# First early pair's Silu behind the output norm's roots, that norm's rows scaled on VectorE, three attention stores issued by ScalarE, in a hybrid encoder layer

## The chip, the cores and the metric

The kernel runs on one core of a Trainium2 chip. Times are device microseconds of one execution of the program; the time of a kernel is the median of several executions. The engines are TensorE (PE in the profile, its weight loads PEld), VectorE (DVE), ScalarE (ACT), GpSimd (POOL) and SyncE (SP), which issues most of the DMA transfers. Each engine takes its instructions from a queue of its own, in the order in which they stand there; an instruction that waits for a semaphore holds all that stand behind it on the same engine. "ACTq" and "SPq" in the profile are the queues' own steps, such as issuing a transfer.

## The reference, cut to what matters

One layer of an encoder on x of 1024 rows of 1024 numbers, all float32:

```python
h = _rms_norm(x, g_mix_pre)
aq, ak, av, dqkv, dgate, dalpha, dbeta = split(h @ w_in)
attn_o = _window_attention(rope(aq), rope(ak), av, sink)   # 8 heads of 64, 2 key heads, blocks of 128 rows
dn_o = _gated_deltanet(dqkv, dgate, dalpha, dbeta, ...)    # 4 heads of 128, both directions
x = x + _rms_norm(concat([attn_o, dn_o]) @ w_out, g_mix_post)
x = x + _rms_norm(cross_attention(_rms_norm(x, g_cross_pre), mem), g_cross_post)
gu = _rms_norm(x, g_ffn_pre) @ w_gate_up
x = x + _rms_norm((silu(gu[:, :2816]) * gu[:, 2816:]) @ w_down, g_ffn_post)
```

`_window_attention` lets each block of 128 rows see itself and its two neighbours: scores, a softmax with a sink term in the denominator, then the product with the values. `_rms_norm` divides a row by the root of its mean square.

## The kernel before

Everything is float32. A matrix product is made of three TensorE products: each operand is split into a rounded "hi" part and the rest "lo" (`split`, L103 on ScalarE makes hi, L104 on VectorE or GpSimd makes lo), and hi·hi, hi·lo and lo·hi are added up in PSUM. Weights are loaded 512 KB at a time into two buffers `wraw` and split into two buffers each of `whi` and `wlo`.

Two places are touched by the change.

**The attention windows beside the delta rule's scan.** `window(n, g)` handles the block n of 128 rows for the key head g (four query heads at once); 16 windows, counted g * NT + n with NT = 8, are run in the order 0 to 15. A window loads its queries (`qr`, L674), splits them (`qs`, L676, L677), makes the scores (`psw`, L685, TensorE), adds the band and takes the row maximum (L687, VectorE), takes the exponential (L694, ScalarE), and multiplies the four score tiles `sc` by the inverse sum `es` (L703 on VectorE or L705 on ScalarE). Its second half transposes them (`ptw`, L711), splits the transposes (`ph`, `pl`) and multiplies with the values (`pow`, L716); `ao` is the sum of two halves of that (L719 on ScalarE, L720 on VectorE) and is stored to `d_mix` (L721). There is one buffer each of `qr` and `ao`, and two PSUM buffers that `psw` and `ptw` take in turn. Windows 0 and 7, 8 and 15 stand at the edge of the sequence: their tiles are 256 wide, the others' 384. The later windows run between the steps of `scan(g)`, the delta rule for two heads in both directions: `psc` is any of its TensorE products, `kv` and `pz` are its loaded operands, L871 on VectorE makes its right-hand side R in place in `kv`, L878 and L880 make `vg` and `vn` of the next product, L891 the new state S. Between these TensorE also makes the memory's keys (`pck`, L983), whose weights GpSimd splits (L104).

**From the norm after cross attention to the feed-forward network.** Two halves of four tiles of 128 rows go through `finish(r, z, eng)`: a root for the output norm (`prs`), the residual added (`xr`, L1352, VectorE) and stored, the sum of squares of the new row (L1355, ScalarE), the root of the next norm (`pr2`, L1343 on ScalarE with the reciprocal L1344 on VectorE), and the row scaled by it (`z`): L1360 on VectorE in the second half of the rows, which is handled first, L1359 on ScalarE in the first half. The rows are then transposed on TensorE (`ptn`, L1459) and combined into sums (L1488 to L1501) that a Strassen-like product needs. While that goes on, TensorE makes five "early" pairs of columns of the gate and up products, which need only the rows that are ready: for each pair two products with the first half of the rows' columns into `pA0` (L1539, 12 matmuls each), which are copied out to `m1` (L1541, ScalarE) and stored, and two that add the second half (L1544). `early_out` then takes Silu of the gate (`sg`, L1524, ScalarE), multiplies with the up product (L1528, VectorE) and stores it. The bank `pA0` of a pair's gate or up is one of four.

ScalarE's roots (Sqrt) and Silu are in different function tables; where the function needed is not in the loaded table, an ACT_TABLE_LOAD stands ahead of it. Copies, Identity and Square are found in each.

What sets the order: the kernel is written in program order, and the builder's scheduler puts each engine's instructions into a queue by a timeline that it works out. `tc.high_priority(AHEAD)` moves the instructions in its block ahead; `tc.issue_after(x.ins)` makes those in its block stand behind x on x's engine. Eight semaphores serve the transfers of all queues in turn ("slots" below): a transfer waits until the one that had its slot eight transfers before has landed, on whichever queue that was.

Of the kernel before, what the change touches and what calls it, by code (L numbers as in the profile page):

```python
# [13 lines left out]
AF = mybir.ActivationFunctionType  # L14
ALU = mybir.AluOpType
# [6 lines left out]
D = 1024  # L22
KT = D // P
NT = S // P
# [4 lines left out]
AHEAD = 300  # L29
# [47 lines left out]
def tile_hybrid_block(  # L77
# [6 lines left out]
    nc = tc.nc  # L84
# [578 lines left out]
    def window(n, g):  # L663

        tok = slice(n * P, (n + 1) * P)
        k0, k1 = max(n - 1, 0), min(n + 1, NT - 1) + 1
        nb = k1 - k0
        w = nb * P
        band = C[:, _AT["band0"] - C0 + (k0 - n + 1) * P:][:, 0:w]

        khi, klo = (t[:, k0 * P:k1 * P] for t in keys[g])
        qr = tw.tile([P, 4, P], F32, tag="qr", name="qr", bufs=1)
        for r in range(2):
            nc.sync.dma_start(qr[64 * r:64 * r + 64], d_q[256 * g:256 * g + 256, tok].rearrange("(h e) t -> e h t", h=4))  # L674
        qs = tw.tile([P, 4, P], F32R, tag="qs", name="qs")
        nc.scalar.copy(qs, qr)  # L676
        nc.gpsimd.tensor_tensor(qs[64:128], qr[64:128], f32(qs[64:128]), ALU.subtract)  # L677

        m4 = tw.tile([P, 4], F32, tag="m4", name="m4")
        ssum = tw.tile([P, 4], F32, tag="ssum", name="ssum")  # L680
        pr = []
        for hh in range(4):
            pp = pw.tile([P, 512], F32, tag="pw", name="psw")
            for i, kk in enumerate((khi, klo)):
                nc.tensor.matmul(pp[:, 0:w], qs[:, hh, :], kk, start=(i == 0), stop=(i == 1))  # L685
            sc = tw.tile([P, 384], F32, tag="sc", name="sc", bufs=8)
            nc.vector.tensor_tensor_reduce(out=sc[:, 0:w], in0=pp[:, 0:w], in1=band, scale=0.125,  # L687
                                           scalar=sink[:, 4 * g + hh:4 * g + hh + 1], op0=ALU.add, op1=ALU.max,
                                           accum_out=m4[:, hh:hh + 1])
            pr.append(sc)  # L690
        nm = tw.tile([P, 4], F32, tag="nm", name="nm")
        nc.vector.tensor_scalar(nm, m4, -1.0, None, ALU.mult)
        for hh in range(4):
            nc.scalar.activation(pr[hh][:, 0:w], pr[hh][:, 0:w], AF.Exp, bias=nm[:, hh:hh + 1],  # L694
                                 accum_out=ssum[:, hh:hh + 1])
        es = tw.tile([P, 4], F32, tag="es", name="es")
        nc.gpsimd.tensor_tensor(es, sink[:, 4 * g:4 * g + 4], m4, ALU.subtract)
        nc.scalar.activation(es, es, AF.Exp)
        nc.vector.tensor_tensor(es, es, ssum, ALU.add)
        nc.vector.reciprocal(es, es)  # L700
        for hh in range(4):
            if not 8 <= g * NT + n < 13:
                nc.vector.tensor_scalar(pr[hh][:, 0:w], pr[hh][:, 0:w], es[:, hh:hh + 1], None, ALU.mult)  # L703
            else:
                nc.scalar.mul(pr[hh][:, 0:w], pr[hh][:, 0:w], es[:, hh:hh + 1])  # L705
        yield
        po = pw.tile([P, 4, P], F32, tag="pow", name="pow", bufs=1)
        for j in range(nb):
            pp = pw.tile([P, 512], F32, tag="pw", name="ptw")
            for hh in range(4):  # L710
                nc.tensor.transpose(pp[:, hh * P:(hh + 1) * P], pr[hh][:, j * P:(j + 1) * P], ident)  # L711
            ph = tw.tile([P, 512], F32R, tag="ph", name="ph")
            pl = tw.tile([P, 512], F32R, tag="pl", name="pl")
            split(ph, pl, pp)
            for i, pe_ in enumerate((ph, pl)):
                nc.tensor.matmul(po.rearrange("p h t -> p (h t)"), vhl[:, k0 + j, g].rearrange("p r e -> p (r e)"), pe_,  # L716
                                 start=(j == 0 and i == 0), stop=(j == nb - 1 and i == 1))
        ao = tw.tile([P, 4, P], F32, tag="ao", name="ao", bufs=1)[0:64]
        nc.scalar.copy(ao, po[64:128])  # L719
        nc.vector.tensor_tensor(ao, po[0:64], ao, ALU.add)  # L720
        nc.sync.dma_start(d_mix[g * 256:(g + 1) * 256, tok].rearrange("(h e) t -> e h t", e=64), ao)  # L721

# [614 lines left out]
        jk = tz.tile([P, HALF], F32, tag="junk", name="junk")  # L1339
        nc.scalar.activation(jk, src, AF.Square, accum_out=ssq[:, ch, r:r + 1])  # L1340

    def inverse_root(rs, ss, scale, bias):
        nc.scalar.activation(rs, ss, AF.Sqrt, bias=bias, scale=scale)  # L1343
        nc.vector.reciprocal(rs, rs)  # L1344

    def finish(r, z, eng):

        tok = slice(r * P, (r + 1) * P)
        xr = res[r]
        rs = tz.tile([P, 1], F32, tag="prs", name="prs", bufs=4)  # L1350
        inverse_root(rs, ssq[:, 1, r:r + 1], 1.0, ssq[:, 0, r:r + 1])
        nc.vector.scalar_tensor_tensor(xr, z, rs, xr, ALU.mult, ALU.add)  # L1352
        nc.sync.dma_start(d_x2[tok, :], xr)
        s2 = tz.tile([P, 1], F32, tag="ps2", name="ps2", bufs=4)
        nc.scalar.activation(z, xr, AF.Square, accum_out=s2)  # L1355
        r2 = tz.tile([P, 1], F32, tag="pr2", name="pr2", bufs=4)
        inverse_root(r2, s2, 1.0 / D, epsc)
        if eng is nc.scalar:
            return nc.scalar.activation(z, xr, AF.Identity, scale=r2)  # L1359
        return nc.vector.tensor_scalar(z, xr, r2, None, ALU.mult)  # L1360

    a11, a12, s3_, a22 = ((q_[0][:, c], q_[1][:, c]) for q_ in (q0, q1) for c in (slice(0, HK), slice(HK, KT)))
    s1_, s4_ = ([r_, [t[:, c] for t in q1]] for r_, c in zip(blocks(raw), (slice(HK, KT), slice(0, HK))))
# [65 lines left out]
        square_of(z[:, HI], 1, r)  # L1429
        gained(z[:, HI], z[:, HI], HI, nc.vector)  # L1430

    scaled = []

    def second_rows(t):
        add(za[:, t], y7[:, t], X[t])
        row_sum(zl[:, t], 4 + t)
        scaled.append(finish(4 + t, zl[:, t], nc.vector))

    def first_half_rows(t):
        add(zz[:, t, HI], e_[:, t], X[t])  # L1440
# [37 lines left out]
                    row_sum(zz[:, t], t)  # L1478
    with tc.issue_after(cut.ins):
        for t in range(4):  # L1480
            finish(t, zz[:, t], nc.scalar)
    tr = LR2.enter_context(pool("tr", 1, side="right"))
    T2, T4 = (blocks(t) for t in operand(opA, "s0"))
    T1, T3 = (blocks(t) for t in operand(opB, "s2"))
# [36 lines left out]
    te = LP.enter_context(pool("te", 2, side="right"))  # L1521

    def early_out(e, sg, A, after=None):
        nc.scalar.activation(sg, A[0], AF.Silu)  # L1524
        with ExitStack() as order_:
            if after:
                order_.enter_context(tc.issue_after(after.ins))
            nc.vector.tensor_tensor(sg, sg, A[1], ALU.mult)  # L1528
        nc.sync.dma_start(d_a["11"][e], sg)

    for e in range(EARLY):
        f = 2 * e
        w, A = [], []
        for i, c0 in enumerate((f * P, FF + f * P)):
            place = fw.tile([P, KT, P], F32, tag=f"fw{i}", name="wraw") if e == EARLY - 1 else None
            whi, wlo = first_gate[i] if e == 0 else load_w(w_gate_up[:, c0:c0 + P], KT, P, place=place)
            w.append(((whi[:, 0:HK], wlo[:, 0:HK]), (whi[:, HK:], wlo[:, HK:])))
            A.append(pg.tile([P, 512], F32, tag="pg", name="pA0"))
            product(A[i], w[i][0], X11)  # L1539
            a1 = te.tile([P, 512], F32, tag="m1", name="m1")  # L1540
            nc.scalar.copy(a1, A[i])  # L1541
            nc.sync.dma_start(d_m1[f + i], a1)
        for i in range(2):
            product(A[i], w[i][1], X21, start=False)  # L1544
# [332 lines left out]
```

## Time and profile before

| | us |
|---|---|
| median of 3 runs | 1521.06 |
| the runs | 1518.25, 1521.06, 1524.97 |
| the profiled execution, whole | 1518.84 |
| its span in the profile | 1516.8 |
| TensorE busy | 1471.5 |
| VectorE busy | 1101.3 |
| ScalarE busy | 784.2 |
| GpSimd busy | 362.8 |

The span is what the profile's rows add up to; 2.0 us of the execution lie outside it. A row of the timeline gives the start from the span's beginning, the duration, the engine, the line, the operation with its tiles (buffer numbers left out), how many instructions in a row it stands for, and, in brackets, how long the engine sat idle before it and what ended that. A row of the table by stretches gives the busy time of each engine in a stretch, the clock that TensorE was granted there (1.00 is full speed) and the share of the sixteen DMA engines' time that transfers took. The windows and the scan run from about 300 to 546 us, the passage to the feed-forward network from 841 to 945 us.

### The profile page before, as it was taken

How to read it: one execution, taken by the hardware profiler on the slowest of the kernel's cores; microseconds unless marked ns; L12 is line 12 of the kernel's file. 1: busy time of each engine (PE TensorE's matmuls, PEld its weight loads, DVE VectorE, ACT ScalarE, POOL GpSimd, SP SyncE). 2: the span in 40 equal slices, each digit the busy share in tenths (PEclk: the TensorE clock that was granted, in tenths of full speed). 3: DMA queues.
4: the chain of work that ended last, by engine and by line, in shares of the span. 5: the costliest groups of instructions: out<-in, count | busy, mean ns of one | idle time of the engine just before them, and what ended most of it. 6: DMA issues, size and time to landing. Idle time of an engine off the chain costs nothing.

```text
span 1516.8 us, 21323 instructions
## 1 busy us (share of the span) xinstructions
PE 1471.5 (97%) x7437; PEld 1239.2 (82%) x7437; DVE 1101.3 (73%) x1801; ACT 784.2 (52%) x1606; POOL 362.8 (24%) x394
## 2 busy tenths in 40 slices
PE   7999999998999999999999998999999999999998
PEld 6888877888989878887788876888888888888787
DVE  5878998676998775538466867776867764696666
ACT  7678844567556764555454684332332332453533
POOL 0011232432325303342201002433524342000030
PEclk9999999999999999999999999999999999999999
DMA  6245554557987584448625553334434333853255
GB/s 203 70 118 142 148 164 129 157 171 193 345 283 234 180 293 158 162 151 262 232 90 180 194 190 123 118 119 132 132 112 152 126 103 116 323 207 97 105 179 168
DMA packets 257751, 256.34 MB, mean 169 GB/s; under 512 B 18128, under 2 KB 190317, under 8 KB 257645
## 3 DMA queue, kind: packets, MB, share of 16 engines
q1 hardware_dynamic: 256493, 252.90, 52.3%
q10 hardware_dynamic: 1152, 2.10, 0.4%
q8 instruction: 58, 0.95, 0.3%
q14 instruction: 48, 0.39, 0.1%
HBM read 178.63 MB, written 73.70 MB: 166 GB/s over the span
## 4 chain that ended last, share of the span: by engine, by line
PE 64%; DVE 8%; DMA 5%; ACT 2%; issue 2%; POOL 1%; SPq 0%; DVEq 0%; ACTq 0%; POOLq 0%
PE pE L1514 8%; PE pD L1514 8%; PE pA L1514 6%; PE pmg L1104 6%; PE pdX L1720 6%; PE pst L1320 5%; PE pdA L1720 4%; PE pB L1514 4%; PE pcq L276 3%; PE psc L843 2%; PE pdD L1720 2%; DMA wpart<-in_w_co_dram 1%; PE pg L276 1%; DMA kv<-d_kv 1%; PE pcv L999 1%
## 5 line engine op out<-in xcount | busy, mean ns | idle before, releaser
L103 ACT CAST whi<-wraw 128x1024 fp32r<-128x1024 f32 x96 | 100.8, 1050 | 120.3 <-DMA wraw<-in_w_gate_up_dram 38.7
L276 PE MATMUL pg<-hlo,whi 128*128 128x512 f32 x352 | 140.0, 398 | 0.0
L276 PE MATMUL pg<-hhi,whi 128*128 128x512 f32 x352 | 139.4, 396 | 0.0
L276 PE MATMUL pg<-hhi,wlo 128*128 128x512 f32 x352 | 139.0, 395 | 0.0
L104 POOL TENSOR_TENSOR wlo<-wraw,whi 128x1024 fp32r<-128x1024 f32 x36 | 87.8, 2441 | 186.4 <-ACT whi L103 182.8
L1514 PE MATMUL pA<-b,whi 128*128 128x512 f32 x352 | 109.8, 393 | 3.6 <-ACT m L1541 2.8
L104 DVE TENSOR_TENSOR wlo<-wraw,whi 128x1024 fp32r<-128x1024 f32 x60 | 74.7, 1245 | 42.2 <-ACT whi L103 38.2
L1514 PEld LDWEIGHTS pA<-b,whi 128*128 128x128 f32 x352 | 65.2, 188 | 18.7 <-ACT m L1541 4.1
L1720 PE MATMUL pdX<-dhl,whi 128*128 128x512 f32 x264 | 76.1, 390 | 1.5 <-ACT dhl L103 0.8
L276 PEld LDWEIGHTS pg<-hhi,whi 128*128 128x128 f32 x352 | 66.5, 189 | 13.4 <-ACT hhi L241 0.3
L276 PEld LDWEIGHTS pg<-hlo,whi 128*128 128x128 f32 x352 | 66.5, 189 | 12.5
L276 PEld LDWEIGHTS pg<-hhi,wlo 128*128 128x128 f32 x352 | 66.5, 189 | 12.5
L1597 POOL TENSOR_TENSOR act<-act,up 128x512 f32<-128x512 f32 x33 | 51.0, 1546 | 82.0 <-DVE up L1596 60.9
L103 ACT CAST whi<-araw 128x1024 fp32r<-128x1024 f32 (+1 forms) x36 | 35.3, 981 | 67.1 <-PE pdX L1720 27.6
L1514 PE MATMUL pA<-b,wlo 128*128 128x512 f32 x176 | 68.8, 392 | 0.5 <-DVE wlo L104 0.5
L104 DVE TENSOR_TENSOR wlo<-araw,whi 128x1024 fp32r<-128x1024 f32 (+1 forms) x36 | 40.7, 1131 | 36.2 <-ACT whi L103 36.1
L1569 POOL TENSOR_TENSOR sr<-wraw 128x512 f32<-128x512 f32 x22 | 29.9, 1359 | 150.6 <-DMA wraw<-in_w_gate_up_dram 88.6
L301 DVE SCALAR_TENSOR_TENSOR acc<-cp,cols,acc 128x1024 f32<-128x1024 f32 x48 | 63.0, 1314 | 0.2
L1720 PEld LDWEIGHTS pdX<-dhl,whi 128*128 128x128 f32 x264 | 49.3, 188 | 12.7 <-ACT dhl L103 1.1
L103 ACT CAST dhl<-b 128x512 fp32r<-128x512 f32 x66 | 40.4, 620 | 31.9 <-PE pdA L1720 13.6
L1514 PE MATMUL pB<-s0h,s1h 128*128 128x512 f32 x176 | 54.4, 390 | 0.7 <-ACT s1h L103 0.7
L103 ACT CAST s0h<-sr 128x512 fp32r<-128x512 f32 x22 | 13.7, 622 | 78.7 <-POOL sr L1569 78.2
(503 smaller groups left out, 4306.1 us busy)
## 6 DMA issues: line engine op xcount, KB each, us to landing
wraw<-in_w_gate_up_dram SPq DMA_DIRECT2D x54, 512.0 KB, 3.8
kv<-d_kv SPq DMA_DIRECT2D x32, 512.0 KB, 7.2
wraw<-in_w_in_dram SPq DMA_DIRECT2D x22, 512.0 KB, 4.0
b<-in_w_down_dram SPq DMA_DIRECT2D x20, 512.0 KB, 6.3
araw<-d_as SPq DMA_DIRECT2D x20, 512.0 KB, 3.6
pz<-d_pz SPq DMA_DIRECT2D x32, 256.0 KB, 6.6
wraw<-in_w_ckv_dram SPq DMA_DIRECT2D x16, 512.0 KB, 4.7
wraw<-in_w_out_dram SPq DMA_DIRECT2D x16, 512.0 KB, 4.5
```

What stands on the lines that cost most here:

```text
L103: nc.scalar.copy(hi, src)
L104: return (eng or nc.vector).tensor_tensor(lo, src, f32(hi), ALU.subtract)
L276: nc.tensor.matmul(p_, w[:, k, :], ah[a][:, k, :], start=(k == 0 and i == 0), stop=(k == nk - 1 and i == 2))
L301: nc.vector.scalar_tensor_tensor(acc, cp[:, t:t + S], taps[t], acc, ALU.mult, ALU.add)
L843: nc.tensor.matmul(out[:, d, h, :], lt[:, d, h, :], rt[:, d, h, :], start=True, stop=True)
L999: nc.tensor.matmul(pp[t], mT[a][:, k, t * P:(t + 1) * P], w[:, kk, :], start=(k == 0 and i == 0), stop=(k == KT - 1 and i == 2))
L1104: nc.tensor.matmul(pp[t], act[a][:, k, tt], w_[:, kk, :], start=(k == 0 and i == 0), stop=(k == KT - 1 and i == 2))
L1320: nc.tensor.matmul(bank, a[:, tt], w, start=(start and i == 0), stop=(stop and i == 2), skip_group_check=not check)
L1514: nc.tensor.matmul(out_, w[a][:, k, :], xx[b_][:, k, :], start=(start and k == 0 and i == 0), stop=(k == HK - 1 and i == 2), skip_group_ch ...
L1569: nc.gpsimd.tensor_tensor(s[0], b_[:, 0:HK], b_[:, HK:], ALU.add)
L1597: nc.gpsimd.tensor_tensor(o_, o_, up, ALU.mult)
L1720: nc.tensor.matmul(banks[t], a[:, k - k0, tt], w, start=(first and k == 0 and i == 0), stop=(k == NB - 1 and i == 2), skip_group_check=not ...
```

## The change

Four edits. Window 7's four score tiles are scaled by ScalarE instead of VectorE. The stores of `ao` of windows 5, 6 and 7 are issued by ScalarE's queue instead of SyncE's. In `finish` the rows of the first half are scaled by VectorE, like those of the second (the local copy of `inverse_root` goes; the outer one at L167, of the same operations, is used), and the last root of that half is returned. Each `early_out`'s Silu is placed behind that root on ScalarE. Last, the copies `m1` are given priority. Nothing is computed otherwise than before.

```diff
@@ window
-            if not 8 <= g * NT + n < 13:
+            if not 7 <= g * NT + n < 13:
                 nc.vector.tensor_scalar(pr[hh][:, 0:w], pr[hh][:, 0:w], es[:, hh:hh + 1], None, ALU.mult)
             else:
                 nc.scalar.mul(pr[hh][:, 0:w], pr[hh][:, 0:w], es[:, hh:hh + 1])
...
-        nc.sync.dma_start(d_mix[g * 256:(g + 1) * 256, tok].rearrange("(h e) t -> e h t", e=64), ao)
+        out_queue = nc.scalar if 5 <= g * NT + n < 8 else nc.sync
+        out_queue.dma_start(d_mix[g * 256:(g + 1) * 256, tok].rearrange("(h e) t -> e h t", e=64), ao)
@@ finish
-        inverse_root(r2, s2, 1.0 / D, epsc)
-        if eng is nc.scalar:
-            return nc.scalar.activation(z, xr, AF.Identity, scale=r2)
-        return nc.vector.tensor_scalar(z, xr, r2, None, ALU.mult)
+        root = inverse_root(r2, s2, 1.0 / D, epsc)
+        nc.vector.tensor_scalar(z, xr, r2, None, ALU.mult)
+        return root
...
     with tc.issue_after(cut.ins):
         for t in range(4):
-            finish(t, zz[:, t], nc.scalar)
+            rooted = finish(t, zz[:, t])
@@ early_out
-        nc.scalar.activation(sg, A[0], AF.Silu)
+        with tc.issue_after(rooted.ins):
+            nc.scalar.activation(sg, A[0], AF.Silu)
@@ early pairs
-            nc.scalar.copy(a1, A[i])
+            with tc.high_priority(AHEAD):
+                nc.scalar.copy(a1, A[i])
```

How the queues stand, before and after. First ScalarE where window 7 is scaled: `sc_3992` to `sc_4007` are window 7's score tiles, `ao_3977` is window 5's output, `ph_4041` and `ph_4052` are parts of window 6, the two `whi` are weights of the memory's keys. Before:

```order
L103 CAST ph_4041<-ptw_4036 128x512
L103 CAST whi_5210<-wraw_5208 128x1024
L103 CAST whi_5397<-wraw_5395 128x1024
L985 COPY cv_4949<-pck_4924 128x256
L103 CAST ph_4052<-ptw_4047 128x512
L719 COPY ao_4058<-pow_4024 64x512
L880 COPY vn_4989<-psc_4982 128x512
L676 CAST qs_4469<-qr_4466 128x512
L103 CAST ph_4247<-ptw_4242 128x512
```

After:

```order
L722 DMA d_mix_113<-ao_3977 64x4x128
L103 CAST whi_5210<-wraw_5208 128x1024
L705 ACTIVATE sc_3992<-sc_3992,es_4015 128x256
L705 ACTIVATE sc_3997<-sc_3997,es_4015 128x256
L705 ACTIVATE sc_4002<-sc_4002,es_4015 128x256
L705 ACTIVATE sc_4007<-sc_4007,es_4015 128x256
L103 CAST whi_5397<-wraw_5395 128x1024
L986 COPY cv_4949<-pck_4924 128x256
L103 CAST ph_4052<-ptw_4047 128x512
L719 COPY ao_4058<-pow_4024 64x512
L881 COPY vn_4989<-psc_4982 128x512
L722 DMA d_mix_113<-ao_4058 64x4x128
```

The four scalings stand between the two weight casts; the store of window 5 stands between `ph_4041` and the first of them, that of window 6 between `vn_4989` and window 7's first `ph_4247`, which is the next row. Both use the same slot as the second half of the scan's load `pz_5257` on SyncE's queue: that half waits for window 5's store, and window 6's store waits for that half.

Second, ScalarE at the first early pair (`sg0_9227`) and the first half's rows (`zz`). Before:

```order
L103 CAST whi_9233<-wraw_9231 128x1024
L1524 ACT_TABLE_LOAD
L1524 ACTIVATE sg0_9227<-pA0_9171 128x512
L103 CAST whi_9255<-wraw_9253 128x1024
L1343 ACT_TABLE_LOAD
L1343 ACTIVATE pr2_9005<-ps2_9003,mhalf_69 128x1
L1355 ACTIVATE zz_8335,ps2_9014<-xr2_8839 128x1024
L1355 ACTIVATE zz_8335,ps2_9025<-xr2_8839 128x1024
L1359 ACTIVATE zz_8335<-xr2_8836,pr2_8994 128x1024
L1343 ACTIVATE pr2_9016<-ps2_9014,mhalf_69 128x1
L1359 ACTIVATE zz_8335<-xr2_8836,pr2_9005 128x1024
L1343 ACTIVATE pr2_9027<-ps2_9025,mhalf_69 128x1
```

After:

```order
L103 CAST whi_9233<-wraw_9231 128x1024
L103 CAST whi_9255<-wraw_9253 128x1024
L168 ACTIVATE pr2_9005<-ps2_9003,mhalf_69 128x1
L1352 ACTIVATE zz_8335,ps2_9014<-xr2_8839 128x1024
L1352 ACTIVATE zz_8335,ps2_9025<-xr2_8839 128x1024
L168 ACTIVATE pr2_9016<-ps2_9014,mhalf_69 128x1
L168 ACTIVATE pr2_9027<-ps2_9025,mhalf_69 128x1
L1519 ACT_TABLE_LOAD
L1519 ACTIVATE sg0_9227<-pA0_9171 128x512
L1537 COPY m1_9250<-pA0_9237 128x512
L1537 COPY m1_9272<-pA0_9259 128x512
L103 CAST whi_9305<-wraw_9303 128x1024
```

Silu stands behind the four roots, with one table load where there were two here (and a third ahead of the second pair's Silu); the scalings L1359 have left the queue.

Third, TensorE at the second early pair (`pA0_9237`, `pA0_9259`), where the first transposes of those rows stand. Before:

```order
L1514 MATMUL pA0_9259<-b0_8907,whi_9255 128x512
L1514 MATMUL pA0_9259<-b3_8909,whi_9255 128x512
L1514 MATMUL pA0_9259<-b0_8907,wlo_9256 128x512
L1459 MATMUL ptn_9041<-ident_68,zz_8335 128x128
L1459 MATMUL ptn_9046<-ident_68,zz_8335 128x128
L1459 MATMUL ptn_9041<-ident_68,zz_8335 128x128
L1459 MATMUL ptn_9046<-ident_68,zz_8335 128x128
L1514 MATMUL pA0_9237<-b0_8908,whi_9233 128x512
```

After:

```order
L1508 MATMUL pA0_9237<-b3_8909,whi_9233 128x512
L1508 MATMUL pA0_9237<-b0_8907,wlo_9234 128x512
L1453 MATMUL ptn_9041<-ident_68,zz_8335 128x128
L1453 MATMUL ptn_9046<-ident_68,zz_8335 128x128
L1508 MATMUL pA0_9259<-b0_8907,wlo_9256 128x512
L1508 MATMUL pA0_9259<-b0_8907,whi_9255 128x512
L1508 MATMUL pA0_9259<-b3_8909,whi_9255 128x512
```

The transposes of the first row tile now stand between the two products of the pair instead of behind both, those of the second behind `pA0_9259`, and those of the third and fourth together after the pair's next product. The later transposes and products of the early pairs are interleaved in another order as well.

8 lines of the change are left out of this document (2 added, 6 removed).

## Prediction, on record before the result

> **What bounds the kernel now.** I read the page's busy times and its chain of waits first, then TensorE's idle time by stretches, then the timelines of the two places that the change touches.
>
> ```profile
> span 1516.8 us, 21323 instructions
> PE 1471.5 (97%) x7437; PEld 1239.2 (82%) x7437; DVE 1101.3 (73%) x1801; ACT 784.2 (52%) x1606; POOL 362.8 (24%) x394
> PE 64%; DVE 8%; DMA 5%; ACT 2%; issue 2%; POOL 1%; SPq 0%; DVEq 0%; ACTq 0%; POOLq 0%
> ```
>
> TensorE is busy for all but 1516.8 − 1471.5 = 45 us, and no edit gives it less work. A gain must come out of those 45 us, or out of stretches in which its clock is low.
>
> ```profile
> 400.00:425.00 25.00, 22.59 (x173) 21.86 (x173) 24.20 (x62) 11.07 (x23) 9.53 (x5) 0.93 1.09 342
> 417.80:420.20 2.40, 0.02 (x1) 0.02 (x1) 2.40 (x5) 0.00 (x0) 1.39 (x1) 1.00 1.02 348
> 420.20:425.50 5.30, 5.30 (x30) 5.16 (x31) 5.30 (x17) 1.17 (x2) 0.00 (x0) 0.68 1.09 367
> 445.00:500.00 55.00, 54.31 (x400) 50.97 (x399) 43.84 (x111) 41.27 (x123) 31.33 (x41) 1.00 0.76 235
> 876.00:886.40 10.40, 7.14 (x30) 4.70 (x29) 4.54 (x8) 10.34 (x16) 0.00 (x0) 1.00 0.78 258
> 886.40:925.50 39.10, 39.10 (x184) 31.98 (x184) 30.75 (x40) 26.41 (x40) 3.35 (x2) 1.00 0.37 121
> 925.50:931.00 5.50, 3.06 (x14) 2.37 (x14) 5.43 (x10) 4.41 (x9) 0.00 (x0) 1.00 0.38 125
> 945.00:1300.00 355.00, 355.00 (x1568) 293.96 (x1567) 252.16 (x300) 103.24 (x168) 133.85 (x84) 1.00 0.39 126
> ```
>
> Columns: stretch, its length, busy time of PE, PE's loads, DVE, ACT, POOL, PE's clock, DMA share, GB/s. Three things stand out. At 417.8 TensorE is idle for 2.4 us while VectorE is busy without a break, and in the 5.3 us behind it its clock is 0.68: 5.3 × 0.32 = 1.7 us of work lost. At 876 to 886.4 TensorE is idle for 3.3 us while ScalarE is busy for 10.34 of 10.40. At 925.5 it is idle for 2.4 us once more. Behind both places TensorE has no room: 54.31 of 55 us, 355 of 355. What it gains, it keeps.
>
> **Window 7's scaling.** These rows are TensorE, VectorE, GpSimd and ScalarE around 418 us.
>
> ```profile
> 420.18 1.27 PE L843 MATMUL psc<-kv,pz 128*128 128x128 f32 x8 [2.41 <-DVE kv L871]
> 421.68 0.41 PE L685 MATMUL psw<-khi,qs 128*128 128x256 f32 x1
> 425.71 0.28 PE L685 MATMUL psw<-klo,qs 128*128 128x256 f32 x1
> 400.92 1.39 DVE L703 TENSOR_SCALAR sc<-sc,es 128x384 f32<-128x384 f32 x4
> 414.84 5.02 DVE L703 TENSOR_SCALAR sc<-sc,es 128x256 f32<-128x256 f32 x4
> 419.79 1.11 DVE L871 SCALAR_TENSOR_TENSOR kv<-psc,nEG,kv 128x128 f32<-128x128 f32 x4
> 414.46 4.74 POOL L104 TENSOR_TENSOR wlo<-wraw,whi 128x1024 fp32r<-128x1024 f32 x2 [2.75 <-ACT whi L103]
> 412.30 1.07 ACT L103 CAST ph<-ptw 128x512 fp32r<-128x512 f32 x2
> 432.41 1.71 ACT L705 ACTIVATE sc<-sc,es 128x256 f32<-128x256 f32 x4 [0.80 <-DVE es L700]
> 426.56 0.58 ACT L103 CAST ph<-ptw 128x512 fp32r<-128x512 f32 x1
> ```
>
> Four scalings of 128x384 take 1.39 us on VectorE; window 7's, of 128x256, take 5.02, and they end just when GpSimd's two splits do. Behind them stands L871, which TensorE waits for. Without them L871 starts about 4.9 us earlier, near 415, and its 1.11 us are over before TensorE arrives at 417.8. The wait of 2.41 goes; with it, if the clock's dip belongs to that wait, go the 1.7 us (the same 256-wide matmul takes 0.41 us in the dip and 0.28 behind it). Together 4.1 us.
>
> ScalarE takes on 1.71 us (the row of window 8, of the same shape). That puts off the second weight cast and window 6's next `ph` by about 2 us. TensorE wants that `ph` behind eight `psc`, near 418.7, and it is then made at about 418.2. I charge 0.8 us for this and similar small waits, between 0 and 2.
>
> **The stores.** Rows: SyncE's and ScalarE's cost of issuing, SyncE's rows of window 5's store and of the load that shares its slot, their times to landing, and VectorE's part of window 6's output.
>
> ```profile
> L721 SPq DMA_DIRECT2D d_mix<-ao x16: 586/602/836, 321.0 to 554.3; - x16
> L817 ACTq DMA_DIRECT2D d_gate<-gt x8: 326/326/371, 261.3 to 359.2; - x8
> 410.12 0.60 SPq L721 DMA_DIRECT2D d_mix<-ao  x1
> d_mix<-ao SPq DMA_DIRECT2D x1, 128.0 KB, 4.7
> 414.88 0.43 SPq L859 DMA_DIRECT2D pz<-d_pz  x1
> pz<-d_pz SPq DMA_DIRECT2D x1, 256.0 KB, 8.2
> 424.26 0.68 DVE L720 TENSOR_TENSOR ao<-pow,ao 64x512 f32<-64x512 f32 x1
> ```
>
> SyncE is relieved of 3 × 0.60 us, which nothing on TensorE's path waits for (no DMA ends a wait of TensorE at 400 to 425): 0. ScalarE pays between 3 × 0.33 (its own issues) and 3 × 0.60 (this store's shape). The waits matter more. Window 5's store now goes out behind the two `ph`, near 413.5 instead of 410.12, and lands 4.7 later, near 418.2. Only then may the second half of `pz` go out, 3.3 us later than its 414.88, and SyncE's queue stands behind it: loads for steps that TensorE reaches 10 us and more later, so 0. Window 6's store then stands on ScalarE until that half of `pz` has landed: it landed at 414.88 + 8.2 = 423.1. The transfers ahead of it are the same, and the DMA share of 1.09 says that it is their volume that it queues behind, so I take 423.1 again; the far end is 418.2 + 8.2 = 426.4. Behind the store stands window 7's first `ph`, at 426.56 today. At 423.1 it is made 3 us earlier than today, before TensorE wants it (425.4 if 3.3 us are gained); at 426.4 the gain of this place is nearly all gone. So the windows give −4.1 + 0.8 = **−3.3 us**, between −4.1 and 0.
>
> **Silu behind the roots.** ScalarE, TensorE, VectorE and GpSimd around 880 us, and TensorE at 928.
>
> ```profile
> 876.89 1.28 ACT L1524 ACT_TABLE_LOAD   x1
> 878.19 0.60 ACT L1524 ACTIVATE sg<-pA 128x512 f32<-128x512 f32 x1
> 879.74 1.28 ACT L1343 ACT_TABLE_LOAD   x1
> 883.32 1.13 ACT L1359 ACTIVATE zz<-xr,pr 128x1024 f32<-128x1024 f32 x1
> 884.60 0.41 PE L1459 MATMUL ptn<-ident,zz 128*128 128x128 f32 x2 [0.97 <-ACT zz L1359]
> 885.82 0.41 PE L1459 MATMUL ptn<-ident,zz 128*128 128x128 f32 x2 [0.81 <-ACT zz L1359]
> 886.38 0.74 PE L1514 MATMUL pA<-b,whi 128*128 128x512 f32 x2 [0.15 <-ACT m L1541]
> 890.29 1.22 DVE L104 TENSOR_TENSOR wlo<-wraw,whi 128x1024 fp32r<-128x1024 f32 x1 [4.23 <-ACT whi L103]
> 859.48 0.75 DVE L1360 TENSOR_SCALAR zl<-xr,pr 128x1024 f32<-128x1024 f32 x1
> 916.20 1.68 POOL L1569 TENSOR_TENSOR sr<-wraw 128x512 f32<-128x512 f32 x1 [49.29 <-DVE wlo L104]
> 927.99 0.73 PE L1514 MATMUL pA<-b,whi 128*128 128x512 f32 x2 [2.44 <-ACT m L1541]
> 927.35 0.58 ACT L1541 COPY m<-pA 128x512 f32<-128x512 f32 x1
> ```
>
> Ahead of the scalings ScalarE now loads two tables and makes a Silu, 2 × 1.28 + 0.60 = 3.2 us, and makes four scalings of 1.13. After the change one load and the Silu stand behind the last root, and the scalings, 4 × 0.75 = 3.0 us, are VectorE's, which sits idle for 4.23 us at one stretch here. They are of the kind that GpSimd held up in window 7, but GpSimd is idle for 49.29 us until 916.20. The first row tile is ready near 879, when TensorE is still at the pair's first product; the fourth behind the Silu's multiplication, near 885, and TensorE wants it behind another 12 matmuls, near 886. So the three waits of 0.97 + 0.81 + 0.15 = 1.9 us go. Silu itself is 3.7 us later; its bank is wanted only by the third pair.
>
> The second term is the 2.44 us at 927.99: TensorE has ended the last early pair's first product and waits for its copy, which stands on ScalarE behind casts that wait for VectorE's sums. VectorE starts its sums about 2.9 us earlier (the rows are ready earlier, and the next pair's split follows), and the new order brings TensorE's transposes forward, which feed them. Then only the copy stands in the way, 0.58 us and some 0.1 to be seen: 2.44 − 0.7 = 1.7 us go. At the other end VectorE, busy for 30.75 of 39.1 us, stays late and nothing goes; at the far good end everything behind, up to the weights that are fetched when VectorE frees their buffer, comes 1.5 us earlier still. I take the middle: −1.9 − 1.7 = **−3.6 us**, between −5.1 and 0. The priority of the copies is in this.
>
> **The sum** is −3.3 − 3.6 = −6.9 us. The profiled execution took 1518.84, 2.2 less than the median of 1521.06; 1518.84 − 6.9 = 1511.9, and against the median 1521.06 − 6.9 = **1514.2 us**. About 0.5%, 7.6 us, is what a measurement here can tell from no change: the forecast lies just inside it.
>
> **Rivals.** *The clock's dip is not the wait's.* For it: the wait of 2.44 us at 927.99 is as long, and the clock stays at 1.00 behind it. Then a dip comes or doesn't by where a wait falls, the runs before did not all have this one, and the change may have another elsewhere. The 1.7 us leave the sum: 1515.9. [...]
>
> *The windows give nothing*, because the transfers are the limit there (DMA share 1.09) and TensorE meets its next operands' landing sooner. Against it: no wait of TensorE there ends with a transfer. −3.6 alone: 1517.5.
>
> *The early pairs give back their gain*, since VectorE stays the last to finish at 931: −3.3 alone, 1517.8.
>
> *ScalarE is held at window 6's store.* This is the one that ends slower. The place is the wait for the second half of `pz`. Up to a landing at 426.4 it costs the windows' gain; from there each microsecond is lost, and the change is slower than before from 426.4 + 3.6 = 430.0. With twice the 8.2 us to landing, 418.2 + 16.4 = 434.6, it is 4.6 us slower: 1525.7. Against it: 8.2 is the longest that I find for `pz` there.
>
> **How the numbers follow.** Forecast 0.50, by its bounds 1511 to 1517; clock 0.15; no gain in the windows 0.17; none in the early pairs 0.08; ScalarE held 0.10. The time is the forecast's. The range runs from 1509 (−9.2, both good ends, and 2.8 that the fastest run lies below the median) to 1522 (no gain and a little); outside are most of the last case and a little below. Faster by over 0.5%, under 1513.5: half of the forecast and a third of the clock's case, 0.30. Slower by over 0.5%, above 1528.7: two thirds of the last case, with holds longer than the one priced, 0.07. Between: 0.63.
>
> **What would show it.** Right: no L703 of window 7 on VectorE; L871 over before TensorE's `psc` at 418, no wait there and a clock of 1.00 at 420 to 425; the transposes at 880 to 886 without a wait; two table loads between 840 and 930 instead of three; less than 1 us ahead of the last early pair's second product. Wrong: ScalarE idle ahead of window 7's first `ph` until a `pz` lands; a new wait of TensorE on `ph` or `vn`; a clock below 1 elsewhere in 400 to 550; a wait of TensorE on a lo part at 890 to 930.

## The result and the profile after

The changed kernel takes 1512.85 us (median of 12, 1509.23 to 1516.22) against 1520.99 for the kernel before: a ratio of 0.9945, 95% interval 0.9932 to 0.9959. The profiled execution after took 1516.22, 3.4 above its median, that of before 2.2 below its own; so the two spans differ by only 2.5 us.

The page's busy times and the chain of waits by engine, after:

```profile
span 1514.3 us, 21323 instructions
PE 1474.7 (97%) x7437; PEld 1240.4 (82%) x7437; DVE 1100.5 (73%) x1801; ACT 778.0 (51%) x1604; POOL 363.0 (24%) x394
PE 64%; DVE 11%; DMA 7%; issue 3%; SPq 1%; ACT 1%; POOL 1%; DVEq 0%; ACTq 0%; POOLq 0%
```

The stretches that the prediction read, after (stretch, its length, busy time of PE, PE's loads, DVE, ACT, POOL, PE's clock, DMA share, GB/s):

```profile
400.00:425.00 25.00, 24.51 (x200) 23.56 (x199) 23.50 (x60) 14.96 (x36) 10.84 (x6) 1.00 1.00 316
417.80:420.20 2.40, 2.40 (x21) 2.32 (x20) 2.30 (x7) 2.40 (x5) 0.95 (x1) 1.00 1.05 409
420.20:425.50 5.30, 5.30 (x43) 4.88 (x42) 4.30 (x16) 3.37 (x7) 3.82 (x2) 1.00 1.07 349
876.00:886.40 10.40, 9.38 (x42) 7.07 (x41) 8.23 (x13) 8.74 (x16) 0.00 (x0) 1.00 0.97 332
886.40:925.50 39.10, 37.91 (x179) 30.76 (x178) 32.29 (x45) 25.16 (x41) 2.96 (x2) 1.00 0.35 115
268.17:275.00 6.83, 6.83 (x21) 5.68 (x22) 2.05 (x1) 2.68 (x6) 2.45 (x4) 0.50 0.91 247
```

The idle 2.4 us at 418 and the clock of 0.68 behind it are gone; at 876 to 886 TensorE is idle for 1.0 us instead of 3.3. The last row is new: 6.83 us at half clock at 268, where the program is the same in both kernels. That low stretch alone costs this execution 3.4 us, and it has nothing to do with the change.

So raw times of two traces can't be subtracted here. For each kernel I take the start of one and the same TensorE matmul less its start in the trace of before, each with half of every low-clock stretch ahead of it taken off ("at full clock"). Worked out that way from the traces, in us:

```
kernel (trace)                   windows: at 400 -> at 448     early pairs: at 870 -> at 959
after                            +0.13 -> +0.06  = -0.07       -0.39 -> -5.00  = -4.61
after, second trace              -1.21 -> -1.45  = -0.24       -1.66 -> -6.30  = -4.64
after, third trace               +0.13 -> -0.07  = -0.20       -0.76 -> -4.97  = -4.21
window 7 on ScalarE alone        -1.20 -> -3.63  = -2.43       -2.95 -> -1.82  = +1.13
stores on ScalarE alone          -0.40 -> +0.76  = +1.16       -0.46 -> -0.80  = -0.34
early pairs alone                -1.30 -> -1.07  = +0.23       -1.32 -> -4.80  = -3.48
after, stores on SyncE (three)   -1.13, -1.09, -1.06           -4.01, -3.53, -4.67
after, window 6's on SyncE       -1.41 -> -2.68  = -1.27       -4.00 -> -8.40  = -4.40
keys' splits on VectorE          +0.95 -> +0.35  = -0.60       -0.12 -> -2.24  = -2.12
after, Silu first                +0.75 -> -1.17  = -1.92       -0.39 -> -2.98  = -2.59
after, rows on ScalarE           -3.26 -> -3.73  = -0.47       -4.90 -> -7.61  = -2.71
```

One trace is one execution, and three kernels whose early pairs are those of before differ there by +1.13, -0.34 and -2.12. All of that arises behind 928: there is a wait for weights at 941 that is longer in some executions, and in the trace of the keys' splits a half-clock stretch at 925 in which the other engines catch up, so that the waits behind it shrink from 1.8 us to 0.35. Up to 940, ahead of the wait for weights, all eight traces with the whole edit of the early pairs gain 4.4 us. The windows give the three traces of the kernel after next to nothing at full clock, and 0.5 and 1.9 us to the last two kernels of the table, whose windows are the same as after; the experiments tell why. The second part of the result is the clock itself. Over 31 executions of the kernel after the mean time is 1513.1 and the mean granted clock 0.9961; over 88 of the kernel before 1520.7 and 0.9938. The span times the clock is 1505.3 against 1509.2, which is 3.9 us; the 0.0023 of clock, on 1515 us, are the other 3.6.

### The profile page after: what moved, and what is told of

It is laid out like the page before. It is cut to its first block, busy times and chain, and to the rows that moved or that the text cites. A ratio compares the mean times of both kernels' runs of the same rounds, so it can differ in the third digit from the quotient of the medians.

```text
span 1514.3 us, 21323 instructions
## 1 busy us (share of the span) xinstructions
PE 1474.7 (97%) x7437; PEld 1240.4 (82%) x7437; DVE 1100.5 (73%) x1801; ACT 778.0 (51%) x1604; POOL 363.0 (24%) x394
## 3 DMA queue, kind: packets, MB, share of 16 engines
q10 hardware_dynamic: 1968, 2.49, 0.5%
## 4 chain that ended last, share of the span: by engine, by line
PE 64%; DVE 11%; DMA 7%; issue 3%; SPq 1%; ACT 1%; POOL 1%; DVEq 0%; ACTq 0%; POOLq 0%
PE pE L1508 8%; PE pD L1508 8%; PE pmg L1105 6%; PE pA L1508 6%; PE pdX L1716 6%; PE pst L1321 5%; PE pB L1508 4%; PE pcq L276 3%; PE psc L844 3%; PE pdA L1716 2%; PE pg L276 2%; PE pdD L1716 2%; DMA wpart<-in_w_co_dram 1%; DMA b<-in_w_down_dram 1%; PE pco L1220 1%
## 5 line engine op out<-in xcount | busy, mean ns | idle before, releaser
L1508 PE MATMUL pD<-x,s3h 128*128 128x512 f32 x176 | 54.2, 389 | 0.0
```

The lines of the kernel that those rows point to most:

```text
L1508: nc.tensor.matmul(out_, w[a][:, k, :], xx[b_][:, k, :], start=(start and k == 0 and i == 0), stop=(k == HK - 1 and i == 2), skip_group_ch ...
```

## The experiments

**What the windows' part is worth by itself, and what the stores are.** Three kernels take the change apart: window 7's scaling alone, the stores alone, and all but both.

```diff
-            if not 8 <= g * NT + n < 13:
+            if not 7 <= g * NT + n < 13:
```

> The kernel before with one edit: window 7's four score tiles scaled by ScalarE; its stores stay on SyncE, the early pairs are as before. Theory (the held store gives the windows' gain back): here no store stands on ScalarE, so window 7's first ph is not held, the wait of 2.4 us at L871 goes and 0.6 us of small waits come, TensorE is ahead by some 2 us behind the window at full clock, and the time falls by 2 to 3.5 us (by the dip of the clock besides), ratio near 0.998. Rival (the transfers are the limit at this place, whatever the stores do): TensorE is ahead by less than 0.5 us behind the window, ratio 0.999 to 1.000. GpSimd theory: VectorE has no scaling left to stall, and no VectorE instruction on SBUF operands alone takes over twice its usual time while GpSimd splits.

Measured: 1515.95 us, ratio 0.9973 (0.9959 to 0.9988). TensorE gains 2.43 us at full clock, more than with the stores moved. GpSimd's, VectorE's and TensorE's rows at the place:

```profile
414.91 4.87 POOL L104 TENSOR_TENSOR wlo<-wraw,whi 128x1024 fp32r<-128x1024 f32 x2 [2.75 <-ACT whi L103]
416.04 1.13 DVE L871 SCALAR_TENSOR_TENSOR kv<-psc,nEG,kv 128x128 f32<-128x128 f32 x4 [0.65 <-PE psc L843]
418.11 1.06 PE L843 MATMUL psc<-kv,pz 128*128 128x128 f32 x8
```

GpSimd works as long as before, but L871 now waits for TensorE rather than TensorE for it, and the `psc` at 418.11 starts without a wait. L871 reads a PSUM tile beside the same splits, and its four take 1.13 us, where they took 1.11 behind the splits in the kernel before.

```diff
-        nc.sync.dma_start(d_mix[...], ao)
+        out_queue = nc.scalar if 5 <= g * NT + n < 8 else nc.sync
+        out_queue.dma_start(d_mix[...], ao)
```

> The kernel before with one edit: the stores of windows 5, 6 and 7 issued by ScalarE. Theory: window 5's store lands some 8 us behind its issue, the second half of the load pz waits for it, and window 6's store waits on ScalarE until that half has landed, with window 7's first ph behind it. Since the wait of 2.4 us at L871 stays here and puts off all else, the hold comes out about as late as ph does today: 0 to +1.5 us, ratio 1.000 to 1.001; an idle stretch of ScalarE of 3 us or more ahead of window 7's ph. Rival (relieving SyncE brings the scan's loads earlier, that is what the window's part gains): -1 to -2 us, ratio 0.999.

Measured: 1520.77 us, ratio 1.0001 (0.9986 to 1.0016): no gain from SyncE's relief is seen. The trace is 1.16 us behind in the windows at full clock, but over the 12 executions the span times the clock is no more than before (1508.6 against 1508.9), so a loss is not shown. ScalarE's idle stretch ahead of window 7's `ph`, expected at 3 us or more, is 1.50 us.

The kernel after, with the two edits above undone, so with the early pairs' part alone:

> The kernel after without its windows' part: window 7's scaling on VectorE and the three stores on SyncE, as before; Silu, the rows' scaling and the copies' priority as after. Theory: the early pairs are worth 4.6 us at full clock, as the two traces show it (TensorE behind by 0.4 us less at 860 and ahead by 5.0 at 945), ratio 0.997, and the waits at 418 and, where the grid of the clock's windows falls that way, the dip behind it stay. Rival (the early pairs and the windows gain only together, or most of the medians' 8.1 us belongs to the windows): 2 us or less, ratio 0.9985 or more. Third view: by the run's clock, a difference that the mean granted clock explains (0.001 of clock is 1.5 us).

Measured: 1515.16 us, ratio 0.9962 (0.9949 to 0.9974). At full clock its trace gains 3.5 us in the early pairs, a little less than expected, because a later wait of 1.75 us near 936 (below) took some of it. The two parts alone make 0.9973 x 0.9962 = 0.9935, where the kernel after, with the stores moved, has 0.9945.

**Does the held store cost the windows' gain?** In the kernel after, ScalarE's and SyncE's rows between window 5's store and window 7's first `ph`, and TensorE's wait for that `ph`:

```profile
414.94 0.66 ACTq L722 DMA_DIRECT2D d_mix<-ao  x1
417.10 1.07 ACT L103 CAST ph<-ptw 128x512 fp32r<-128x512 f32 x2
423.32 0.32 SPq L860 DMA_DIRECT2D pz<-d_pz  x1
428.93 0.61 ACTq L722 DMA_DIRECT2D d_mix<-ao  x1
429.64 0.58 ACT L103 CAST ph<-ptw 128x512 fp32r<-128x512 f32 x1 [4.26 <-PE psc L844]
430.28 0.50 PE L716 MATMUL pow<-ph,vhl 128*128 128x512 f32 x1 [0.52 <-ACT ph L103]
```

Window 5's store goes out at 414.94, the second half of `pz`, which needs its slot, at 423.32, and window 6's store, which needs that half's, at 428.93. ScalarE is idle for 4.26 us, and TensorE waits behind it. Window 5's store stands in the queue behind the two `ph` of 417.10, and yet it went out 2.2 us before they began: the queue issued it ahead of arithmetic that stands before it, so that its instructions did not all start in the order in which they stand. The third trace of the same kernel has it plainer, and names the transfer:

```profile
412.01 0.67 ACTq L722 DMA_DIRECT2D d_mix<-ao  x1
427.12 0.58 ACTq L722 DMA_DIRECT2D d_mix<-ao  x1
427.80 0.59 ACT L103 CAST ph<-ptw 128x512 fp32r<-128x512 f32 x1 [5.35 <-DMA pz<-d_pz]
428.44 0.50 PE L716 MATMUL pow<-ph,vhl 128*128 128x512 f32 x1 [1.61 <-ACT ph L103]
```

The kernel after with all three stores back on SyncE's queue, in three comparisons, the last two beside the kernel after itself:

> The kernel after with the three stores back on SyncE: nothing else changes but the order of window 7's first ph and the next window's qs on ScalarE. Theory: the 1.8 us that the after kernel gives back between 424 and 434 us are the held store's, so this is faster than the after kernel by 1 to 2 us: ratio to the kernel before 0.993 against 0.9945, ScalarE not idle for over 2 us ahead of window 7's ph. Rival (relieving SyncE is part of the gain): slower than the after kernel by 1 us or more, ratio 0.995 to 0.996.

> The kernel after itself, once more, beside its variants. Both theories: 1512.5 to 1513, ratio 0.9945. A second trace of it: by the theory of the held store ScalarE is idle for some 4 us ahead of window 7's first ph again, and TensorE gives back 1 to 2 us at full clock between 424 and 434 us; if that hold was one execution's, it is under 2 us here.

> The kernel after with the three stores on SyncE, once more and on the same chip as the kernel after. Theory (held store): 1 to 2.5 us faster than it, 1510.5 to 1511.5. Rival (the first comparison, of six executions, was chance): equal to it within 0.7 us.

> The kernel after, a third time, beside its variant without the three stores on ScalarE. Theory: 1512.5 to 1513.5; ScalarE idle for some 4 us ahead of window 7's first ph, as in the two traces of it so far.

> The kernel after with the three stores on SyncE, a third time. The two traces of it are ahead of the two of the kernel after by 0.9 us in the windows' place at full clock. Theory: 1 to 2 us faster than the kernel after, 1511 to 1512. Rival: the same within 0.7 us.

Measured, stores on SyncE: 1510.49, 1511.87 and 1512.27 us, ratios 0.9928 (0.9905 to 0.9951), 0.9942 (0.9920 to 0.9965) and 0.9944 (0.9925 to 0.9963). The kernel after: 1512.52 and 1513.82 us, ratios 0.9951 (0.9934 to 0.9967) and 0.9952 (0.9934 to 0.9969). The variant is ahead each time, by 0.65 us (within the rival's 0.7) and 1.55 where both ran side by side; over all executions (20 and 31) the means differ by 1.5 us with a standard error of 0.8, which doesn't settle it. The span times the clock, which takes the dips out, does: 1503.3 against 1505.3, 2.0 us with a standard error of 0.5, and 1.9 and 2.0 side by side.

The traces show where it is lost. Five of them have window 7's scaling and window 6's store on ScalarE. Times are in the time of the kernel before, each trace laid on it at the matmul at 400; the gains are at full clock.

| trace | window 5's store | second half of `pz` | window 6's store | gain at 428 | gain left at 434 |
|---|---|---|---|---|---|
| after | 411.39 | 419.77 | 425.38 | 1.20 | 0.07 |
| after, second | 411.39 | 419.69 | 425.20 | 1.19 | 0.25 |
| after, third | 410.18 | 417.21 | 425.29 | 2.41 | 0.20 |
| after, Silu first | 409.47 | 417.48 | 423.56 | 2.44 | 1.92 |
| after, rows on ScalarE | 411.36 | 419.38 | 425.01 | 1.23 | 0.47 |

In each the gain left is 425.5 less the time of window 6's store, to within 0.1 us: what the store comes later, the windows lose. In the five traces with window 6's store on SyncE the gain at 434 is what it was at 428. The hold costs 0.5 to 2.2 us.

Which link costs? Window 6's store alone is put back on SyncE:

```diff
-        out_queue = nc.scalar if 5 <= g * NT + n < 8 else nc.sync
+        out_queue = nc.scalar if g * NT + n in (5, 7) else nc.sync
```

> The kernel after with window 6's store alone back on SyncE; windows 5 and 7 are stored by ScalarE, so window 5's store still goes out as late as in the kernel after and the second half of pz still waits for it, but nothing on ScalarE waits for that half. Theory (it is ScalarE's own hold that costs): as fast as with all three on SyncE, 1510.5 to 1511.5, no idle stretch of ScalarE over 2.5 us ahead of window 7's ph. Rival (it is the late loads that cost, the hold is only seen): as slow as the kernel after, 1512.5 to 1513.

Measured: 1511.49 us (6 executions), ratio 0.9935 (0.9910 to 0.9960), and 1.27 us gained in the windows, like the kernel with all three on SyncE. Window 7's first `ph` has no idle time ahead of it; these are ScalarE's rows there, and SyncE's of the second half of `pz`:

```profile
411.60 0.67 ACTq L722 DMA_DIRECT2D d_mix<-ao  x1
419.40 0.32 SPq L860 DMA_DIRECT2D pz<-d_pz  x1
422.92 0.62 ACT L676 CAST qs<-qr 128x512 fp32r<-128x512 f32 x1 [0.87 <-PE psw L685]
423.44 0.58 ACT L103 CAST ph<-ptw 128x512 fp32r<-128x512 f32 x1
```

Window 5's store still goes out on ScalarE, and the half of `pz` still only 7.8 us behind it. So it is the engine that is held, not the late loads on SyncE, that costs.

**Is it GpSimd that makes window 7's scaling slow?** The kernel before with the two weight splits beside it on VectorE:

```diff
-        whi, wlo = load_w(w_ckv[:, ct * P:(ct + 1) * P], KT, P, nc.gpsimd)
+        whi, wlo = load_w(w_ckv[:, ct * P:(ct + 1) * P], KT, P, nc.vector if ct in (3, 4) else nc.gpsimd)
```

> The kernel before with the two weight splits of the memory's keys that run beside window 7's scaling made by VectorE instead of GpSimd; the scaling itself stays on VectorE. Theory (the 5.02 us of the four scalings are GpSimd's work beside them): the four scalings take 1.0 to 1.4 us, one split of 1.2 us stands ahead of them, so L871 starts 2.5 us earlier and the wait of TensorE ahead of psc falls from 2.4 to under 0.5 us; ratio 0.997 to 0.999. Rival (256-wide tiles there are slow for a reason of their own): the four scalings still take 4 us or more, the wait grows by the 1.2 us of the split, ratio 1.000 or more.

Measured: 1518.67 us, ratio 0.9982 (0.9965 to 1.0000). VectorE's rows at the place:

```profile
413.99 1.22 DVE L104 TENSOR_TENSOR wlo<-wraw,whi 128x1024 fp32r<-128x1024 f32 x1
415.12 1.13 DVE L703 TENSOR_SCALAR sc<-sc,es 128x256 f32<-128x256 f32 x4
416.17 1.12 DVE L871 SCALAR_TENSOR_TENSOR kv<-psc,nEG,kv 128x128 f32<-128x128 f32 x4
```

The same four scalings, 5.02 us beside GpSimd's splits, take 1.13 without them, though VectorE does one split more ahead of them. The inference of the prediction is shown. Taken one by one, the scalings of the kernel before show how: the first two end 0.15 us behind one split of GpSimd each, the other two take 0.34.

```profile
414.46 2.38 POOL L104 TENSOR_TENSOR wlo<-wraw,whi 128x1024 fp32r<-128x1024 f32 x1 [2.75 <-ACT whi L103]
416.80 2.40 POOL L104 TENSOR_TENSOR wlo<-wraw,whi 128x1024 fp32r<-128x1024 f32 x1
414.84 2.15 DVE L703 TENSOR_SCALAR sc<-sc,es 128x256 f32<-128x256 f32 x1
416.91 2.43 DVE L703 TENSOR_SCALAR sc<-sc,es 128x256 f32<-128x256 f32 x1
419.26 0.34 DVE L703 TENSOR_SCALAR sc<-sc,es 128x256 f32<-128x256 f32 x1
```

The wait at 418 is gone in this kernel; the gain is small in part since VectorE's second split makes TensorE wait elsewhere (0.75 us for a row maximum).

**Which half of the early pairs' edit works?** First Silu back where it was, the rows left on VectorE; then the rows back on ScalarE, Silu left behind the roots.

```diff
-        with tc.issue_after(rooted.ins):
-            nc.scalar.activation(sg, A[0], AF.Silu)
+        nc.scalar.activation(sg, A[0], AF.Silu)
```

> The kernel after without the place of Silu: it stands where the kernel before has it, ahead of the roots, with three table loads; the rows stay on VectorE. Theory (both halves are needed: ScalarE has to make the roots early and be rid of the scalings): the roots come 3.2 us later than in the kernel after, VectorE's rows with them, and TensorE waits 1 to 2 us between 878 and 888; at 945 TensorE is ahead by 2.5 to 3.5 us instead of 4.6 at full clock; ratio 0.9955 to 0.9965. Rival (the scalings alone were it): no wait there over 0.5 us, ratio 0.9945 to 0.995. Other rival (Silu's place alone was it): the early pairs gain under 1 us, ratio 0.998.

```diff
-        nc.vector.tensor_scalar(z, xr, r2, None, ALU.mult)
+        if eng is nc.scalar:
+            nc.scalar.activation(z, xr, AF.Identity, scale=r2)
+        else:
+            nc.vector.tensor_scalar(z, xr, r2, None, ALU.mult)
...
-            rooted = finish(t, zz[:, t])
+            rooted = finish(t, zz[:, t], nc.scalar)
```

> The kernel after with the first half's rows scaled by ScalarE again, Silu behind the roots with one table load. Theory (both halves are needed): the four scalings of 1.13 us are on ScalarE's path again, Silu stands between the second and the third, the copies m1 behind; TensorE waits about 1 us between 880 and 890, VectorE's sums are 1 to 2 us later than in the kernel after, and some of the wait at 925 is back; at 945 ahead by 2 to 3.5 us; ratio 0.9955 to 0.9965. Rival (Silu's place alone was it): no wait over 0.5 us, ratio 0.9945 to 0.995. Other rival (the scalings alone were it): under 1 us gained, ratio 0.998.

Measured: 1516.30 us, 0.9971 (0.9954 to 0.9988), and 1514.20 us, 0.9969 (0.9952 to 0.9986); at full clock 2.6 and 2.7 us gained in the early pairs instead of some 4.4. The intervals of the ratios leave out the rival near 0.995 and hold both the theory and the rival at 0.998; the traces, with more than 1 us gained, rule that one out. Each half alone brings more than half of the gain. With Silu first, TensorE waits for 0.58 us between 878 and 888, for a copy `m1`, instead of 1 to 2; with the rows on ScalarE it waits 1.38 us for a copy `m1` that stands behind a scaling, and the wait ahead of the last pair's second product is 0.72 as in the kernel after, where the theory had some of it back. In the order Silu first (one row), rows on ScalarE (two):

```profile
882.23 0.73 PE L1508 MATMUL pA<-b,whi 128*128 128x512 f32 x2 [0.58 <-ACT m L1536]
879.94 2.20 ACT L1356 ACTIVATE zz<-xr,pr 128x1024 f32<-128x1024 f32 x2
880.11 0.73 PE L1511 MATMUL pA<-b,whi 128*128 128x512 f32 x2 [1.38 <-ACT m L1540]
```

## Why the prediction came out right, and where its terms were off

**The time.** The forecast was 1514.2 us; 1512.85 was measured, 8.1 us off the kernel before instead of 6.9. It is reached by other amounts than the sum had.

**The windows, −3.3 forecast, −0.1 to −0.2 at full clock in the traces of the kernel after.** The wait of 2.41 went and the clock's dip with it; L871 is over before TensorE comes. At full clock the wait was worth 2.7 us in every kernel with window 7 on ScalarE. The small waits, charged at 0.8 us (0 to 2), are of two kinds: 0.2 to 0.3 in the traces of window 7 alone, of Silu first and the third of the kernel after, and 1.4 to 1.6 in the others, so that 2.4 or 1.1 to 1.3 us are left ahead of the store. The two differ, with the same queues up to this place, by when a load `qr` lands for which ScalarE waits: in the second kind 1 to 2 us later against TensorE, and all that stands behind on ScalarE, the scalings and the next `ph`, is late with it. The same kernel has both kinds; what decides when the load lands stays open.

The store was the step that failed in size. The prediction put window 5's store at 413.5 and its landing at 418.2, where the second half of `pz` would go out. The store went out earlier, at 409.5 to 411.4, and that half only 7.0 to 8.4 us behind it, not 4.7; the two errors nearly cancel, and `pz` goes out at 417.2 to 419.8. What was too short is the rest: from there to window 6's store the prediction took 4.9 us, since the half of `pz` would land at 423.1 again, with 8.2 as the far end. It is 5.5 to 8.1. Window 6's store goes out at 425.0 to 425.4 in four of five traces, and there nearly all of the gain is gone (the prediction had that point at 426.4; it is 425.5). The mechanism was priced, as the rival that ends slower and as the bound of 0; the far end was the likely one. So "the windows give nothing" came true at full clock, though not for the reason that this rival named, the transfers as a limit: with the stores on SyncE the same transfers leave 1.1 us.

**The early pairs, −3.6 forecast, −4.4 measured up to 940 and −3.5 to −4.7 behind the wait for weights.** Rows of the kernel after: the one table load, the transposes of the first two row tiles, which have no wait, and the two waits at the last pair.

```profile
881.82 1.28 ACT L1519 ACT_TABLE_LOAD   x1
882.07 0.38 PE L1453 MATMUL ptn<-ident,zz 128*128 128x128 f32 x2
884.59 0.38 PE L1453 MATMUL ptn<-ident,zz 128*128 128x128 f32 x2
921.94 0.50 PE L1508 MATMUL pA<-b,wlo 128*128 128x512 f32 x1 [0.47 <-DVE wlo L104]
925.23 0.73 PE L1508 MATMUL pA<-b,whi 128*128 128x512 f32 x2 [0.72 <-ACT m L1537]
```

The waits for the first rows (1.9 us) went. The wait ahead of the last pair's second product fell from 2.44 to 0.72, the 1.7 us that were priced. A new wait on a lo part, named as a sign against, does come (0.47). These rows make 3.1 us. Two waits for a split, ahead of the rows (0.52 to 0.22) and behind the pairs (0.54 to 0.31), which the sum didn't have, are 0.5 us shorter. For the other 0.8 there is only an estimate: a wait that goes brings some 0.3 us more than its row says, as at 418, where 2.41 us of idle time were worth 2.7, and three went.

Behind the pairs TensorE waits for weights, 0.4 to 2.2 us in most of the traces, the longer the later the transfer lands; this is why the earlier start did not always stay a gain. It is not the edit's: the trace of window 7 alone, with the early pairs as before, has 2.07 us there. This is the longest, in the second trace of the kernel with the stores on SyncE:

```profile
932.90 0.62 ACT L103 CAST bhi<-wraw 128x512 fp32r<-128x512 f32 x1 [5.79 <-DMA wraw<-in_w_gate_up_dram]
937.25 1.01 PE L1507 MATMUL pB<-s0h,s1h 128*128 128x512 f32 x2 [2.18 <-ACT s1h L103]
```

The count of table loads was wrong by one: two are left between 840 and 930, but there had been four. The copies' priority, put under this term, costs and brings nothing: without it every engine's order is the same.

**The clock, −1.7 forecast, about −3.6 measured.** The rival said that the dip comes by where a wait falls. That is so (last section), and it cuts both ways. The same wait at 418 has no dip in the trace of the stores alone; but the early pairs of the kernel before have dips at 884 and 942 in the trace of window 7 alone, and at 925 in that of the keys' splits. The step that was missing is that the waits at 884 and 925 have a chance of a dip too (each in one of the four traces with these pairs as before); the sum had a dip only where the one profiled execution showed one. Ten traces with the edit of the early pairs, or half of it, have no dip at either place. The wait for weights stays, and its dip with it: in two of the ten, at 938. The executions show how much each edit brings: the mean granted clock is 0.9937 in the 29 executions of before beside which the parts ran, 0.9949 with window 7 on ScalarE alone, 0.9935 with the stores alone and 0.9948 with the early pairs alone. That is 1.9 us for window 7, near the 1.7 of the forecast, and 1.8 for the early pairs, for which the forecast had nothing; each has a standard error of some 0.7.

**What made the time come out.** Without the dip's 1.7 us the sum had 5.2 us at full clock, of which 1.6 in the windows; the means show 3.9, and the windows next to nothing. The clock gave 3.6 instead of 1.7. That these two misses, of some 1.5 and 1.9 us, nearly cancel is luck.

**What the time does not separate.** The chances put more on "within 0.5%" than on "faster"; the ratio lies at that bound, 0.55% with an interval of 0.41 to 0.68.

## What to carry to other kernels

A store that is moved onto a compute engine's queue brings that queue the store's waits, its shared DMA slot above all (ScalarE sat idle for 4.26 us here); price it by the time from issue to the next use of the slot, as measured where the transfers are as dense as there (DMA share about 1 here), and look at what stands behind it. A VectorE operation on tiles in SBUF can last until a GpSimd operation beside it ends (2.15 and 2.43 us instead of 0.34 here), so moving one of the two can be worth more than the operation's own time. Price a wait of TensorE of 1.5 us or more (it can leave a stretch of 3.41 us busy for only some 55%; of 17 stretches busy for 44 to 55%, 10 were followed by half clock, next section) with the chance of a half-clock stretch behind it, also where the profiled execution shows none.

## What the runs showed of the hardware

**The clock followed a fixed grid in each trace.** In every trace the low stretches are 3.41 us long, or twice that, at clock 0.50, and those of one trace start a whole number of 3.413 us apart (in the trace of before at 366.69, 421.30 and 537.35: 16 and 34 steps); only the last, at the program's end, is of another length (5.58 us in the trace of before, 5.91 in that of after). Where the grid stands differs from execution to execution: a stretch begins at 417.89 in the trace of before and at 415.85 in that of the stores alone. Three stretches of that grid with their successors: in the kernel before at 418 and at 926, and at 416 in the kernel with the stores alone (same columns as above):

```profile
417.89:421.30 3.41, 1.12 (x9) 1.12 (x9) 3.41 (x10) 0.00 (x0) 1.30 (x1) 1.00 1.01 363
421.30:424.71 3.41, 3.41 (x17) 3.27 (x16) 3.41 (x11) 1.17 (x2) 0.00 (x0) 0.50 1.11 361
...
923.06:926.47 3.41, 2.49 (x11) 1.71 (x10) 3.38 (x5) 1.95 (x4) 0.77 (x1) 1.00 0.00 0
926.47:929.88 3.41, 1.89 (x8) 1.59 (x9) 3.41 (x6) 2.61 (x5) 0.00 (x0) 1.00 0.30 89
929.88:933.29 3.41, 2.87 (x12) 1.91 (x12) 3.38 (x7) 1.76 (x3) 0.00 (x0) 1.00 0.94 302
```

```profile
415.85:419.26 3.41, 1.52 (x13) 1.28 (x11) 3.41 (x4) 0.59 (x1) 2.96 (x2) 1.00 1.06 353
419.26:422.67 3.41, 2.82 (x19) 2.58 (x20) 3.41 (x13) 0.55 (x1) 0.00 (x0) 1.00 1.10 366
```

At 418 TensorE was busy for 1.12 of the 3.41 us, and the next stretch runs at half. The equal wait at 926 lies across two stretches, busy for 2.49 and 1.89: no dip. The same wait of 2.4 us in the kernel with the stores alone leaves 1.52 busy (45%), and no dip either. Over all 14 traces (the first and last 30 us left out), a stretch in which TensorE was busy for under 44% was followed by half clock 21 times of 21; with 44 to 55%, 10 of 17; with 55 to 75%, 7 of 114. All of these seven lie at one place of the program, at 242 to 265 us, and five times a low stretch in which TensorE was busy for 86 to 100% was followed by a second one: busy time alone does not decide it, and what else does stays open.

**VectorE beside GpSimd.** Four scalings of 128x256 took 5.02 us beside GpSimd's splits and 1.13 without; two of the four ended 0.15 us behind the end of one split each, after 2.15 and 2.43 us instead of 0.34. What makes them last that long, no run here shows.
